# A hybrid decoder layer in one kernel: the order of a chunk's products, value tiles in halves of channels, transposes in eights, and one shifted tile

## The chip, the cores and the metric

The kernel runs on one core of a Trainium2 chip. Its time is device microseconds from launch to end; a lower time is better. The core has TensorE (PE, with the weight loads PEld beside it), VectorE (DVE), ScalarE (ACT), GpSimd (POOL), and SyncE (SP), which issues most of the DMAs. Each engine works its own instructions through in order and waits at semaphores for the others.

## The reference

One layer of a decoder trunk is computed for 2048 prompt tokens and for 8 separate sample tokens, all in float32. The normalised and modulated input `hn` goes through one input product whose columns are split into an LRU group (a convolution over 4 tokens, gates, a linear recurrence) and a group of gated linear attention (GLA) with 4 heads. Both are concatenated and go through one output product:

```python
hn = _rmsnorm(x, g_norm) * (1.0 + scale[:, None]) + shift[:, None]
z = hn @ w_in
xa, za, q, k, v, glr, zg = jnp.split(z, SPLITS, axis=-1)
...
def step(S, xs):
    qn, kn, vn, dl = xs
    o = jnp.einsum('bhck,bhkv->bhcv', qn, S)
    S = jnp.exp(dl[:, :, 0, :])[..., None] * S + jnp.einsum('bhck,bhcv->bhkv', kn, vn)
    return S, o
...
o = (o_intra + o_inter)...
mix = jnp.concatenate([y_lru, y_gla], axis=-1) @ w_out
x = x + gate[:, None] * mix
```

The model width is 1024, a head has 128 key and 256 value channels. The state `S` of a head (128 x 256) is carried from chunk to chunk: a chunk's output is the product inside the chunk (`o_intra`, masked attention times values) plus the query times the state (`o_inter`).

## The kernel before

**Numbers and products.** A float32 product is made of three products of rounded parts: high times high, high times low, low times high. So `project` (L661 to L663: projections with 128 weight columns at a time) and `value_mm` (L346 to L348: values, tokens on the partitions) issue three matmuls for each of the 8 channel tiles. The parts of `hn` are `hh` and `hl`. The weights come by SP in tiles `w`, three buffers in rotation (L293 issues such a load, split beforehand into parts); a load into a buffer waits on SP for the last instruction that read the buffer, and all later DMAs of SP wait behind it.

**Halves.** The 2048 tokens go in two halves of 1024. Half 0 runs to about 600 us, half 1 to about 1100 us, and the output product follows. In a half, each head (order 3, 0, 1, 2) has its key, value and query projections, and then segments of chunks of 128 tokens; between them run the LRU tiles. Between the halves `hn` of the second half must be put into `hh` and `hl`.

**Who sets the order.** A scheduler puts the instructions of each engine in order from the program's order and its own estimates. The program paces the GLA chunks by units of work (`tick`, `after`) and mixes small work into the projections: `drips` is a list of small steps, and `drip` takes one after every second channel tile of a projection.

**Accumulators.** PSUM gives `acc` four buffers (projections, values), `tp` two (transposes), and one bank each to `pkv` and `po`, the two results of a GLA chunk.

**The places of the change.**
- `gla_chunk` (L1059 on) is called 64 times, and 60 times with a carried state. It issues three products into `pkv` (keys times values: L1068 to L1070), three into `po` (masked attention `amh`, `aml` times values: L1072 to L1074) and the product of the query with the state, in float32, two passes (L1076). Then DVE adds `pkv` to the state (L1077), scales it (L1078) and copies `po` out (L1081). Before the first chunk of a segment, DVE makes the rests of the keys and of the attention, `kTl` (L1052) and `aml` (L1049), and scales the state (L1056).
- `values` (L933 on) multiplies 8 token tiles by a head's value weights, which lie in two `w` tiles, one for the channel tiles 0 to 3 and one for 4 to 7. In half 1 the last two token tiles are interleaved: both take the first half of the channels, then both the second. ACT (L957) and DVE (L958) take each result out. The next weights that SP loads are the query's.
- `next_hn` (L1428) calls `modulate`, which transposes two token tiles of the normalised second tokens for pairs of channel tiles (four transposes L197 for a pair), lets ACT (L199, L201) or DVE (L203) modulate, POOL round (L204, `hh`) and DVE subtract (L205, `hl`). `lru_last_a` puts these calls, one for each pair of channel tiles and each of four groups `g` of 256 tokens, into `drips`, so that they run inside the projections of the last LRU tile of half 0. Behind them come the sums of `hn` parts (L1491, L1495, L1500) for a Strassen product (L1559, about 600 to 620 us).
- `wq` (L471) holds the first query weights, a tile of the start.

Of the kernel before, what the change touches and what calls it, by code (L numbers as in the profile page):

```python
# [8 lines left out]
F32 = mybir.dt.float32  # L9
F32R = mybir.dt.float32r  # L10
# [4 lines left out]
P = 128  # L15
D = 1024
KT = D // P
# [4 lines left out]
DK = 128  # L22
DV = 256
# [3 lines left out]
XA, ZA, Q0, K0, V0, GLR, ZG = 0, 1024, 2048, 2560, 3072, 4096, 4112  # L27
# [11 lines left out]
HEADS = (3, 0, 1, 2)  # L39
# [15 lines left out]
def hybrid_kernel(ctx, tc, i, o):  # L55
# [7 lines left out]
    def acc():  # L63
        return psum.tile([P, 512], F32, tag="acc", name="acc", bufs=4)
# [41 lines left out]
    amh = cp.tile([P, 4, P], F32R, name="amh")  # L106
# [80 lines left out]
    def modulate(xt, g, kts):  # L187

        c = slice(g * 256, (g + 1) * 256)
        for k2 in range(kts[0], kts[1], 2):  # L190
            pt = tps().rearrange("p (k t) -> p k t", k=2)
            cg = slice(g % 2 * 256, g % 2 * 256 + 256)
            f = (fs4[(1, 2, 0)[k2 // 4 if g < 2 else 2]][:, k2 % 4:k2 % 4 + 2, cg] if g < 2 or k2 >= 4
                 else ra[k2 // 2][:, :, cg])
            for kt in range(2):
                for j in range(2):
                    PE.transpose(pt[:, kt, j * P:(j + 1) * P],  # L197
                                 xt[j][:, (k2 + kt) * P:(k2 + kt + 1) * P], ident)
            S.activation(f[:, 0], pt[:, 0], AF.Identity, scale=Gm[:, k2, 8:9], bias=Sh[:, k2, 8:9])  # L199
            if g < 3:  # L200
                S.activation(f[:, 1], pt[:, 1], AF.Identity, scale=Gm[:, k2 + 1, 8:9], bias=Sh[:, k2 + 1, 8:9])  # L201
            else:
                V.tensor_scalar(f[:, 1], pt[:, 1], Gm[:, k2 + 1, 8:9], Sh[:, k2 + 1, 8:9], op0=OP.mult, op1=OP.add)  # L203
            G.tensor_scalar(hh[:, k2:k2 + 2, c], f, 1.0, 0.0, op0=OP.mult, op1=OP.add)  # L204
            V.tensor_tensor(hl[:, k2:k2 + 2, c], f, hh[:, k2:k2 + 2, c].bitcast(F32), op=OP.subtract)  # L205
# [76 lines left out]
    def weights(col, n, k0=0, nk=KT, both=None, later=False, pieces=1):  # L282


        q = 48 if n == DV else 0
        c = slice(q, q + nk * n)
        if both is None:
            both = wp.tile([P, 2, 1088], F32R, tag="w", name="w", bufs=3)
        hi, lo = [both[:, j, c].rearrange("p (k n) -> p k n", n=n) for j in range(2)]
        known = (col, k0) in parts  # L290
        raw = None
        if known:
            SP.dma_start(both[:, :, c].bitcast(F32), parts[col, k0])  # L293
        else:
            raw = wp.tile([P, 1088], F32, tag="wr", name="wr")[:, :nk * n].rearrange("p (k n) -> p k n", n=n)
            for k in range(0, nk, nk // pieces):
                r = slice(k, k + nk // pieces)
                load = lambda r=r: SP.dma_start(raw[:, r], i["w_in"][
                    0, (k0 + r.start) * P:(k0 + r.stop) * P, col:col + n].rearrange("(k p) n -> p k n", p=P))
                loads.append(load) if k else load()  # L300
        split = []
        for k in range(0, nk, nk // pieces):
            r = slice(k, k + nk // pieces)
            split += [lambda r=r: S.copy(hi[:, r], raw[:, r]),
                      lambda r=r: V.tensor_tensor(lo[:, r], raw[:, r], hi[:, r].bitcast(F32), op=OP.subtract)]
        if not known:
            splits.extend(split)
            if not later:
                split_parts()
            parts[col, k0] = dpool.tile([P, 2, nk * n], F32, tag=f"w{col}_{k0}", name="parts")  # L310
            stores.append((parts[col, k0], both[:, :, c].bitcast(F32)))
            if not later:
                store_parts()
        return hi, lo, raw
# [28 lines left out]
    def value_mm(ps, c, w, n, kts):  # L343
        for kt in range(*kts):
            hi, lo, _ = w[kt // 4]
            PE.matmul(ps, hh[:, kt, c], hi[:, kt % 4], start=kt == 0, stop=False)  # L346
            PE.matmul(ps, hh[:, kt, c], lo[:, kt % 4], start=False, stop=False)  # L347
            PE.matmul(ps, hl[:, kt, c], hi[:, kt % 4], start=False, stop=kt == KT - 1)  # L348
            if kt % 2:
                drip()  # L350
# [86 lines left out]
    with tc.tile_pool(name="ada", bufs=1, side="right") as ap:  # L437
# [30 lines left out]
        xt45 = [xp.tile([P, TH + NS], F32, tag="xt", name="xt")[:, :D] for t in range(2)]  # L468
        for t in range(2):
            SP.dma_start(xt45[t], i["x_prompt"][0, (4 + t) * P:(5 + t) * P])  # L470
        wkq0.append(weights(Q0 + HEADS[0] * DK, DK, both=st.tile([P, 2, D], F32R, name="wq"), later=True))  # L471
        x67 = x_pair(2)
        for t in range(2):
            SP.dma_start(x67[t], i["x_prompt"][0, (6 + t) * P:(7 + t) * P])
# [458 lines left out]
    def values(half, h, w):  # L933
        first = h == HEADS[0]
        n = DV + (RANK if first else 0)
        vh, vl = new_values()
        turns = []
        for tt in range(8):
            if half == 1 and tt == first:
                with held(V) if first else ExitStack():  # L940
                    raw = raw_values(h, n)
            if tt == 4:
                while drips:
                    drip()
            if half == 0 or tt < 6:
                ps = acc()
                value_mm(ps[:, :n], slice(tt * P, (tt + 1) * P), w, n, (0, KT))
            elif tt == 6:
                both = [acc(), acc()]
                for k in (0, 4):  # L950
                    for m in range(2):
                        value_mm(both[m][:, :n], slice((6 + m) * P, (7 + m) * P), w, n, (k, k + 4))
                ps = both[0]
            else:
                ps = both[1]
            hi, lo = vh[tt // 4][:, tt % 4], vl[tt // 4][:, tt % 4]
            S.copy(hi, ps[:, :DV])  # L957
            V.tensor_tensor(lo, ps[:, :DV], hi.bitcast(F32), op=OP.subtract)  # L958
            if len(turns) == 3 or tt == 7 and turns:
                turns.pop(0)()  # L960
            if first:
                turns.append(low_rank(ps[:, DV:n], slice(0, P), tt * P))
            tick(0.5)
        if half == 1:
            turns.append(sample_values(h, raw, n))
        for f in turns:
            after(1, f, True)
        return vh, vl
# [90 lines left out]
    def gla_chunk(half, h, s, c, prep, run, v):  # L1059

        qi, _, f, _ = prep
        kT, on, ss = run
        first = half == 0 and s == 0 and c == 0
        t = slice(c * P, (c + 1) * P)
        pkv = psum.tile([P, 512], F32, tag="kv", name="pkv", bufs=1)[:, :DV]
        tt = SEGS[half][s][0] // P + c
        vh, vl = [x[tt // 4][:, tt % 4] for x in v]
        PE.matmul(pkv, kT[0][:, t], vh, start=True, stop=False)  # L1068
        PE.matmul(pkv, kT[0][:, t], vl, start=False, stop=False)
        PE.matmul(pkv, kT[1][:, t], vh, start=False, stop=True)  # L1070
        po = psum.tile([P, 512], F32, tag="o", name="po", bufs=1)[:, :DV]
        PE.matmul(po, amh[:, c], vh, start=True, stop=False)  # L1072
        PE.matmul(po, amh[:, c], vl, start=False, stop=False)
        PE.matmul(po, aml[:, c], vh, start=False, stop=first)  # L1074
        if not first:
            PE.matmul(po, qi[:, t], St[h], start=False, stop=True)  # L1076
            V.tensor_tensor(St[h], St[h], pkv, op=OP.add)  # L1077
            V.tensor_scalar(St[h], St[h], f[:, c + 1:c + 2], None, op0=OP.mult)  # L1078
        else:
            V.tensor_scalar(St[h], pkv, f[:, c + 1:c + 2], None, op0=OP.mult)  # L1080
        V.tensor_copy(on[:, c], po)  # L1081
        square_sum(xp, ss[:, c:c + 1], on[:, c], P, DV)
# [344 lines left out]

    def next_hn(xt, g, k):  # L1428

        modulate(xt[g], g, (k, k + 2))  # L1430
        if (g, k) == (1, 0):
            normalize(xp, xt[3])

    def lru_last_a(js):

        xa_load, xa_unit, za_load, za_unit = lru_units(0)
        xt = [hn_load(0)]
        lru(0, js[:-2])
        outw["stop"] = True
        lru(0, js[-2:-1])  # L1440
        t = xa_load(js[-1])
        za_load(t)
        flush_gla()
        while outw["busy"]:
            heapq.heappop(pend)[2]()
        open_sp()
        xt += [hn_load(1), hn_load(2), hn_load(3, False)]
        for s in range(2):
            xa_unit(t, s)
            za_unit(t, s)  # L1450
            for g in range(2 * s, 2 * s + 2):
                for k in range(0, KT, 2):
                    drips.append(lambda g=g, k=k: next_hn(xt, g, k))

    spx = ExitStack()
    sp_ = None
# [802 lines left out]
```

## Time and profile before

| | |
|---|---|
| time, median of 3 runs | 1449.03 us (1447.66 to 1450.63) |
| the profiled execution | 1449.01 us, of which the span 1447.2 us |
| PE busy | 1420.5 us, 98% |
| DVE busy | 1049.8 us, 73% |
| ACT busy | 690.2 us, 48% |
| POOL busy | 219.4 us, 15% |
| granted TensorE clock, mean | 0.997 |

The span is the time between the first and the last instruction. PE's matmuls overlap in the records: where a row has a duration of 0.28 us and the next starts 0.12 us later, 0.12 is what the matmul costs. I call the distance from one start to the next the step. A row of the timeline ends with the idle time before it and what ended that. A row of the waits names who waited, at which line, for whom.

### The profile page before, as it was taken

To read this page: it belongs to the slowest core of one execution; us is meant where nothing else is said; L and a number is where in the kernel's file an instruction comes from. 1 tells how busy PE (TensorE), PEld (TensorE's weight loads), DVE (VectorE), ACT (ScalarE), POOL (GpSimd) and SP (SyncE) were. 2 spreads that over 40 slices of the span, in tenths; PEclk is the share of its full clock that TensorE was granted. 3 is DMA by queue.
4 is the path that set the end of the run, shared out by engine and by line. 5 is a ranking of instruction groups with operands and counts; after the bars stand their busy time and mean duration, and the time that the engine had idled before them with its cause. 6 is when DMAs were issued, how large, how long until landed. Compare 5 with 4: busy or idle time off the path is not lost. (4 is left out here: it accounts for less than half of the span.)

```text
span 1447.2 us, 23571 instructions
## 1 busy us (share of the span) xinstructions
PE 1420.5 (98%) x8741; PEld 1248.7 (86%) x8741; DVE 1049.8 (73%) x2473; ACT 690.2 (48%) x1251; POOL 219.4 (15%) x364
## 2 busy tenths in 40 slices
PE   7999999999999999999999999999999999999998
PEld 6888989899898988878899999999998887778886
DVE  5757658776676688955458688596888986688886
ACT  4644544663445358624353454635567622144342
POOL 0200212122122013100111422333210000000000
PEclk9999999999999999999999999999999999999999
DMA  9755785874565546577844675655671767694453
GB/s 331 267 186 175 258 266 190 258 244 153 192 220 190 171 173 216 186 241 236 287 148 145 205 238 172 229 196 181 237 253 68 288 226 272 228 355 138 137 168 117
DMA packets 161753, 305.33 MB, mean 211 GB/s; under 512 B 12963, under 2 KB 91459, under 8 KB 159198
## 3 DMA queue, kind: packets, MB, share of 16 engines
q1 hardware_dynamic: 106837, 217.39, 44.1%
q0 software_dynamic: 22752, 70.44, 14.1%
q10 hardware_dynamic: 32048, 16.00, 3.7%
q8 instruction: 69, 1.13, 0.3%
q14 instruction: 47, 0.38, 0.1%
HBM read 188.51 MB, written 115.33 MB: 210 GB/s over the span
## 5 line engine op out<-in xcount | busy, mean ns | idle before, releaser
L661 PE MATMUL acc<-hh,w 128*128 128x512 f32 (+3 forms) x1112 | 385.7, 347 | 3.0 <-DMA w<-parts 1.8
L663 PE MATMUL acc<-hh,w 128*128 128x512 f32 (+3 forms) x1112 | 375.8, 338 | 0.0
L662 PE MATMUL acc<-hl,w 128*128 128x512 f32 (+3 forms) x1112 | 375.1, 337 | 0.2 <-DVE hl L205 0.2
L661 PEld LDWEIGHTS acc<-hh,w 128*128 128x128 f32 x1112 | 209.2, 188 | 21.7 <-DVE f L1005 1.6
L662 PEld LDWEIGHTS acc<-hl,w 128*128 128x128 f32 x1112 | 209.3, 188 | 16.7 <-DVE hl L205 0.5
L663 PEld LDWEIGHTS acc<-hh,w 128*128 128x128 f32 x1112 | 209.1, 188 | 16.5
L1845 PE MATMUL acc<-w,a 128*128 128x512 f32 (+1 forms) x792 | 184.8, 386 | 0.0
L1845 PEld LDWEIGHTS acc<-w,a 128*128 128x128 f32 x792 | 146.8, 188 | 33.2 <-issue 3.4
L346 PE MATMUL acc<-w,hh 128*128 128x256 f32 (+1 forms) x508 | 143.8, 283 | 0.1
L348 PE MATMUL acc<-w,hl 128*128 128x256 f32 (+1 forms) x508 | 142.8, 281 | 0.2 <-DVE hl L228 0.2
L347 PE MATMUL acc<-w,hh 128*128 128x256 f32 (+1 forms) x508 | 142.7, 281 | 0.0
L1845 PE MATMUL tp<-w,a 128*128 128x512 f32 x564 | 136.3, 391 | 0.0
L1845 PEld LDWEIGHTS tp<-w,a 128*128 128x128 f32 x564 | 105.2, 188 | 27.2 <-issue 5.1
L346 PEld LDWEIGHTS acc<-w,hh 128*128 128x128 f32 x508 | 95.6, 188 | 1.3 <-ACT zs L1129 0.4
L348 PEld LDWEIGHTS acc<-w,hl 128*128 128x128 f32 x508 | 96.0, 189 | 0.4 <-DVE hl L228 0.4
L347 PEld LDWEIGHTS acc<-w,hh 128*128 128x128 f32 x508 | 95.5, 188 | 0.2
L1129 ACT ACTIVATE zs<-acc 128x512 f32<-128x512 f32 (+3 forms) x70 | 34.4, 491 | 110.1 <-PE acc L663 105.0
L1695 ACT CAST a<-s 128x512 fp32r<-128x512 f32 x61 | 36.5, 620 | 95.1 <-issue 34.5
L1278 DVE SCALAR_TENSOR_TENSOR cv<-xa,vecT,cv 128x512 f32<-128x512 f32 (+2 forms) x120 | 76.6, 641 | 5.5 <-ACT cv L1276 5.1
L1130 DVE SCALAR_TENSOR_TENSOR zs<-zs,acc 128x512 f32<-128x512 f32 (+3 forms) x70 | 38.5, 550 | 45.7 <-ACT zs L1129 45.7
L957 ACT CAST vh<-acc 128x256 fp32r<-128x256 f32 x56 | 20.5, 370 | 85.9 <-PE acc L348 68.0
L958 DVE TENSOR_TENSOR vl<-acc,vh 128x256 fp32r<-128x256 f32 x56 | 23.4, 420 | 47.1 <-ACT vh L957 46.9
(409 smaller groups left out, 2745.2 us busy)
## 6 DMA issues: line engine op xcount, KB each, us to landing
parts<-w SPq DMA_DIRECT2D x37, 1024.0 KB
w<-parts SPq DMA_DIRECT2D x28, 1024.0 KB
wr<-in_w_in_dram SPq DMA_DIRECT2D x38, 512.0 KB
a<-mixd SPq DMA_DIRECT2D x63, 256.0 KB
w<-wd SPq DMA_DIRECT2D x12, 1024.0 KB
w<-twd SPq DMA_DIRECT2D x20, 512.0 KB
mixd<-zs ACTq DMA_DIRECT2D x34, 256.0 KB
wada<-in_w_ada_dram SPq DMA_DIRECT2D x16, 512.0 KB
```

What stands on the lines that cost most here:

```text
L346: PE.matmul(ps, hh[:, kt, c], hi[:, kt % 4], start=kt == 0, stop=False)
L347: PE.matmul(ps, hh[:, kt, c], lo[:, kt % 4], start=False, stop=False)
L348: PE.matmul(ps, hl[:, kt, c], hi[:, kt % 4], start=False, stop=kt == KT - 1)
L661: PE.matmul(ps[:, :n], hi[:, kt], a, start=kt == 0, stop=False)
L662: PE.matmul(ps[:, :n], hi[:, kt], b, start=False, stop=False)
L663: PE.matmul(ps[:, :n], lo[:, kt], a, start=False, stop=kt == KT - 1)
L958: V.tensor_tensor(lo, ps[:, :DV], hi.bitcast(F32), op=OP.subtract)
L1129: S.activation(z, ps, AF.Tanh, scale=0.5)
L1130: V.scalar_tensor_tensor(z, z, 1.0, ps, op0=OP.add, op1=OP.mult)
L1278: V.scalar_tensor_tensor(cv[:, cq], xa[:, cq.start + k:cq.stop + k], cw[k], cv[:, cq], op0=OP.mult, op1=OP.add)
L1695: S.copy(t[:, 0, k], (low(t) if src is None else src)[:, k])
L1845: PE.matmul(ps, t[:, u, k], w[:, v, k, c], start=(q < 3 or ps is own) and (k, u, v) == (0, 0, 0), stop=(k, u) == (3, 1), skip_group_check= ...
```

## The change

Four edits, independent of each other.

1. In `gla_chunk` the state's product opens the accumulation in `po` and stands before the products of `pkv`; the attention's products close it.
2. In `values` of half 1 the last three token tiles instead of the last two are interleaved by halves of the channels.
3. `next_hn` handles four channel tiles in a call (eight transposes) instead of two, and an empty step follows each in `drips`, so that as many steps stand in the list as before.
4. The tile of the first query weights is 56 floats longer, and the weights begin behind these 56 floats (224 bytes), which shifts them and the tiles allocated after them in the start's pool.

```diff
-        wkq0.append(weights(Q0 + HEADS[0] * DK, DK, both=st.tile([P, 2, D], F32R, name="wq"), later=True))
+        wkq0.append(weights(Q0 + HEADS[0] * DK, DK, both=st.tile([P, 2 * D + 56], F32R, name="wq")[:, 56:].rearrange("p (j n) -> p j n", j=2), later=True))
...
-            if half == 0 or tt < 6:
+            if half == 0 or tt < 5:
                 ps = acc()
                 value_mm(ps[:, :n], slice(tt * P, (tt + 1) * P), w, n, (0, KT))
-            elif tt == 6:
-                both = [acc(), acc()]
-                for k in (0, 4):
-                    for m in range(2):
-                        value_mm(both[m][:, :n], slice((6 + m) * P, (7 + m) * P), w, n, (k, k + 4))
-                ps = both[0]
             else:
-                ps = both[1]
+                if tt == 5:
+                    three = [acc() for _ in range(3)]
+                    for k in (0, 4):
+                        for m in range(3):
+                            value_mm(three[m][:, :n], slice((5 + m) * P, (6 + m) * P), w, n, (k, k + 4))
+                ps = three[tt - 5]
...
+        po = psum.tile([P, 512], F32, tag="o", name="po", bufs=1)[:, :DV]
+        if not first:
+            PE.matmul(po, qi[:, t], St[h], start=True, stop=False)
         PE.matmul(pkv, kT[0][:, t], vh, start=True, stop=False)
         PE.matmul(pkv, kT[0][:, t], vl, start=False, stop=False)
         PE.matmul(pkv, kT[1][:, t], vh, start=False, stop=True)
-        po = psum.tile([P, 512], F32, tag="o", name="po", bufs=1)[:, :DV]
-        PE.matmul(po, amh[:, c], vh, start=True, stop=False)
+        PE.matmul(po, amh[:, c], vh, start=first, stop=False)
         PE.matmul(po, amh[:, c], vl, start=False, stop=False)
-        PE.matmul(po, aml[:, c], vh, start=False, stop=first)
+        PE.matmul(po, aml[:, c], vh, start=False, stop=True)
         if not first:
-            PE.matmul(po, qi[:, t], St[h], start=False, stop=True)
             V.tensor_tensor(St[h], St[h], pkv, op=OP.add)
...
-        modulate(xt[g], g, (k, k + 2))
+        modulate(xt[g], g, (k, k + 4))
...
-                for k in range(0, KT, 2):
-                    drips.append(lambda g=g, k=k: next_hn(xt, g, k))
+                for k in range(0, KT, 4):
+                    drips.extend([lambda g=g, k=k: next_hn(xt, g, k), lambda: None])
```

PE, one chunk of half 0. Before (`S_117` is the state, `xb` the query, L1042 the next transposes of the attention):

```order
L1068 MATMUL pkv<-vh,kTh 128x256
L1069 MATMUL pkv<-vl,kTh 128x256
L1070 MATMUL pkv<-vh,kTl 128x256
L1072 MATMUL po<-vh,amh 128x256
L1073 MATMUL po<-vl,amh 128x256
L1074 MATMUL po<-vh,aml 128x256
L1076 MATMUL po<-S_117,xb 128x256
```

After, with the line numbers of the changed kernel (L1069 there is the state's product):

```order
L1069 MATMUL po<-S_117,xb 128x256
L1070 MATMUL pkv<-vh,kTh 128x256
L1071 MATMUL pkv<-vl,kTh 128x256
L1072 MATMUL pkv<-vh,kTl 128x256
L1073 MATMUL po<-vh,amh 128x256
L1074 MATMUL po<-vl,amh 128x256
L1075 MATMUL po<-vh,aml 128x256
```

The state's product moved from the end of the chunk's seven to its head, and with it the first use of `po`.

DVE, during the last LRU tile of half 0, up to the sum L1130 that frees an accumulator near 577 us (L1278 is the convolution, L147 to L153 a reciprocal root in short steps). Before; ahead of these rows stand an L1278 and an L205:

```order
L1278 SCALAR_TENSOR_TENSOR cv<-xa,vecT,cv 128x512
L147 TENSOR_SCALAR rs_x<-ss 128x2
L1278 SCALAR_TENSOR_TENSOR cv<-xa,vecT,cv 128x512
L148 TENSOR_SCALAR rs_t<-rs_x 128x2
L1385 COPY xa<-xac 128x3
L149 TENSOR_SCALAR rs_y<-rs_t 128x2
L151 TENSOR_TENSOR rs_t<-rs_y 128x2
L205 TENSOR_TENSOR hl<-fs_5824,hh 128x2x256
L152 SCALAR_TENSOR_TENSOR rs_t<-rs_t,rs_x 128x2
L153 SCALAR_TENSOR_TENSOR rs_y<-rs_t,rs_y 128x2
L1130 SCALAR_TENSOR_TENSOR zs<-zs,acc 128x512
```

After; ahead of these rows stand an L1278, an L205, an L1278 and another L205:

```order
L1278 SCALAR_TENSOR_TENSOR cv<-xa,vecT,cv 128x512
L147 TENSOR_SCALAR rs_x<-ss 128x2
L1385 COPY xa<-xac 128x3
L148 TENSOR_SCALAR rs_t<-rs_x 128x2
L149 TENSOR_SCALAR rs_y<-rs_t 128x2
L151 TENSOR_TENSOR rs_t<-rs_y 128x2
L152 SCALAR_TENSOR_TENSOR rs_t<-rs_t,rs_x 128x2
L153 SCALAR_TENSOR_TENSOR rs_y<-rs_t,rs_y 128x2
L205 TENSOR_TENSOR hl<-fs_5828,hh 128x2x256
L151 TENSOR_TENSOR rs_t<-rs_y 128x2
L152 SCALAR_TENSOR_TENSOR rs_t<-rs_t,rs_x 128x2
L1130 SCALAR_TENSOR_TENSOR zs<-zs,acc 128x512
```

Between the first of the three L1278 and L1130 now stand three L205 instead of two, and more of the short steps.

DVE, the end of the same turns, about 586 to 596 us. Before:

```order
L203 TENSOR_SCALAR ra<-tp,Gm,Sh 128x256
L205 TENSOR_TENSOR hl<-ra,hh 128x2x256
L1130 SCALAR_TENSOR_TENSOR zs<-zs,acc 128x256
L203 TENSOR_SCALAR ra<-tp,Gm,Sh 128x256
L205 TENSOR_TENSOR hl<-ra,hh 128x2x256
L203 TENSOR_SCALAR fs_5823<-tp,Gm,Sh 128x256
L205 TENSOR_TENSOR hl<-fs_5823,hh 128x2x256
L1130 SCALAR_TENSOR_TENSOR zs<-zs,acc 128x256
L203 TENSOR_SCALAR fs_5823<-tp,Gm,Sh 128x256
L1500 TENSOR_TENSOR fs_5823<-fs_5823,ra 128x1024
L205 TENSOR_TENSOR hl<-fs_5823,hh 128x2x256
L1330 SCALAR_TENSOR_TENSOR tx<-tx,cv 128x1024
```

After:

```order
L203 TENSOR_SCALAR ra<-tp,Gm,Sh 128x256 x2
L205 TENSOR_TENSOR hl<-ra,hh 128x2x256 x2
L1130 SCALAR_TENSOR_TENSOR zs<-zs,acc 128x256
L203 TENSOR_SCALAR fs_5823<-tp,Gm,Sh 128x256 x2
L205 TENSOR_TENSOR hl<-fs_5823,hh 128x2x256 x2
L1130 SCALAR_TENSOR_TENSOR zs<-zs,acc 128x256
L1330 SCALAR_TENSOR_TENSOR tx<-tx,cv 128x1024
L1500 TENSOR_TENSOR fs_5823<-fs_5823,ra 128x1024 x2
```

Pairs of L203 and L205 that alternated now stand two by two, and both L1500 stand together behind L1330.

## The prediction

> **What bounds the kernel now.** I read the page first, then the waits of PE, then the timelines of the places that the change touches. The page, with PE's share, its slices and its granted clock:
>
> ```profile
> span 1447.2 us, 23571 instructions
> PE 1420.5 (98%) x8741; PEld 1248.7 (86%) x8741; DVE 1049.8 (73%) x2473; ACT 690.2 (48%) x1251; POOL 219.4 (15%) x364
> PE   7999999999999999999999999999999999999998
> PEclk9999999999999999999999999999999999999999
> ```
>
> PE is the bound from end to end. The change leaves PE's instructions as many and as large as they were, so it can move the time in two ways only: what PE waits for, and how fast a matmul runs. The profiled execution took 1449.01 us (span 1447.2), 0.02 from the median of the runs, 1449.03; my sum is made against 1449.0 and needs no correction. A difference under 0.2% (2.9 us) can hardly be told from none.
>
> These rows of PE's waits (us in total, times, longest) are those that the change can reach; the last is that of PE's weight loads:
>
> ```profile
> PE acc L661 <- DMA w<-parts: 1.8, 2, 1.3
> PE acc L1559 <- DVE so L1495: 1.4, 2, 1.2
> PE po L1072 <- DVE on L1081: 0.9, 2, 0.7
> PE acc L661 <- DVE zs L1130: 0.9, 1, 0.9
> PE acc L1559 <- DVE ra L1495: 0.8, 1, 0.8
> PE pkv L1070 <- DVE kTl L1052: 0.8, 3, 0.3
> PE acc L662 <- DVE hl L205: 0.2, 1, 0.2
> PEld po L1072 <- DVE on L1081: 3.3, 10, 1.0
> ```
>
> They are small: 6.8 us of idle without the last row. No outcome of tens of microseconds is in sight unless the change makes a wait that isn't there.
>
> **The value tiles (values, half 1).** The queue SP loads the next query weights (L293) into a buffer of `w` that the first half of the channels of the value weights still holds; it waits for the last matmul that reads it. Two of these loads, and what PE does when it reaches them:
>
> ```profile
> 818.06 0.52 SPq L293 DMA_DIRECT2D w<-parts  x1
> 825.80 0.33 PE L662 MATMUL acc<-hl,w 128*128 128x384 f32 x1
> 825.97 0.34 PE L663 MATMUL acc<-hh,w 128*128 128x384 f32 x1
> 827.60 0.41 PE L661 MATMUL acc<-hh,w 128*128 128x384 f32 x1 [1.29 <-DMA w<-parts]
> ...
> 907.99 0.52 SPq L293 DMA_DIRECT2D w<-parts  x1
> 915.90 0.34 PE L663 MATMUL acc<-hh,w 128*128 128x384 f32 x1
> 916.77 0.41 PE L661 MATMUL acc<-hh,w 128*128 128x384 f32 x1 [0.53 <-DMA w<-parts]
> ```
>
> PE's step there is 0.17 (825.80 to 825.97), so the stalls cost 827.60 - 825.97 - 0.17 = 1.46 and 916.77 - 915.90 - 0.17 = 0.70. With two tiles in halves, the first half of the channels is read for the last time 24 matmuls (4 channel tiles x 3 x 2 tiles) before the end of the values; with three tiles, 36. The load may go out 12 matmuls earlier. A matmul of 128x256 steps 0.12 (753.53 to 753.65 in the fence below; 264 wide there), so 1.4 us. The landing lies 9.5 and 8.8 us behind the issue; if it moves with the issue, the first stall shrinks to about 0.1 and the second is gone: **-2.1**. The other two heads show no such wait and gain nothing. The bounds: 0, if the transfer meets others and lands no earlier, and -2.2. The three evictions that now come close together (L957, L958) feed chunks that begin much later, and four accumulators are enough for three open ones, so they cost nothing; if they were late, the next projection would wait for an accumulator, at most the 0.4 us of one L958.
>
> **The state's product first (gla_chunk).** Sixty chunks issue it, in two passes. A chunk without waits, then the second chunk of a segment, then the first chunk of the next segment:
>
> ```profile
> 752.97 0.59 PE L1076 MATMUL po<-S,xb 128*128 128x256 f32 x2
> 753.53 0.29 PE L662 MATMUL acc<-hl,w 128*128 128x264 f32 x1
> 753.65 0.28 PE L663 MATMUL acc<-hh,w 128*128 128x264 f32 x1
> ...
> 756.54 0.28 PE L1070 MATMUL pkv<-vh,kTl 128*128 128x256 f32 x1
> 756.95 0.38 PE L1072 MATMUL po<-vh,amh 128*128 128x256 f32 x1
> ...
> 852.61 0.28 PE L1069 MATMUL pkv<-vl,kTh 128*128 128x256 f32 x1
> 853.15 0.38 PE L1070 MATMUL pkv<-vh,kTl 128*128 128x256 f32 x1 [0.27 <-DVE kTl L1052]
> ```
> ```profile
> 756.48 0.42 DVE L1081 COPY on<-po 128x256 f32<-128x256 f32 x1
> 851.64 0.34 DVE L1056 TENSOR_SCALAR S<-S,f 128x256 f32<-128x256 f32 x1
> 852.55 0.55 DVE L1052 TENSOR_TENSOR kTl<-tp,kTh 128x384 fp32r<-128x384 f32 x1
> ```
>
> The product costs 753.53 - 752.97 - 0.12 = 0.44 us wherever it stands. What moves is when PE asks for its inputs. The bank `po` is single: it is free when the copy L1081 of the chunk before has ended. Now three products of `pkv` (3 x 0.12 = 0.36 us) run ahead of that demand; afterwards none. At 756.54 PE waits until the copy's end (756.48 + 0.42 = 756.90): step 0.41, so 0.29 lost. It will wait 0.36 longer. That place occurs once in each of four heads (756, 847, 936, 1025 us): **+1.4**. Against it, at the first chunk of a second segment (852, 941, 1031 us) PE waits for kTl: 853.15 - 852.61 - 0.12 = 0.42, with further steps of about 0.4 for kTh and aml; there S is ready (851.64 + 0.34 = 851.98, while pkv begins at 852.38), so 0.44 us of product come ahead and fill those gaps, and the amh group no longer has to wait: net -0.46 a head, **-1.4**. Of the other chunks the waits above name few: 2 matmuls and 10 weight loads in 64 chunks waited for L1081. In half 0 the timelines show S and the copy ready at least 0.3 us before `pkv` begins, so these cost nothing but about 0.2 at 506 us, where DVE's order changes; a handful of chunks in half 1 that already stand late gain 0.1 to 0.2 each in the same way as at 852, by my estimate -0.8. Together 1.4 - 1.4 + 0.2 - 0.8 = **-0.6**, between -2.0 (the gaps filled, no new wait) and +1.8 (no gap filled, four longer waits).
>
> **The turns of next_hn in eights.** As many transposes in fewer, larger groups. The stall at 577 us, and the four waits of DVE for POOL's cast near the end of these turns:
>
> ```profile
> 576.85 0.60 PE L197 MATMUL tp<-ident,xst 128*128 128x128 f32 x4
> 578.37 0.39 PE L661 MATMUL acc<-hh,w 128*128 128x256 f32 x1 [0.92 <-DVE zs L1130]
> ...
> 576.76 0.68 DVE L205 TENSOR_TENSOR hl<-fs,hh 128x512 fp32r<-128x512 f32 x1
> 577.36 0.15 DVE L152 SCALAR_TENSOR_TENSOR rs_t<-rs_t,rs_x 128x2 f32<-128x2 f32 x1
> 577.63 0.69 DVE L1130 SCALAR_TENSOR_TENSOR zs<-zs,acc 128x512 f32<-128x512 f32 x1
> ...
> 587.78 0.69 DVE L205 TENSOR_TENSOR hl<-ra,hh 128x512 fp32r<-128x512 f32 x1 [0.81 <-POOL hh L204]
> 590.07 0.69 DVE L205 TENSOR_TENSOR hl<-ra,hh 128x512 fp32r<-128x512 f32 x1 [0.81 <-POOL hh L204]
> 592.03 0.69 DVE L205 TENSOR_TENSOR hl<-fs,hh 128x512 fp32r<-128x512 f32 x1 [0.81 <-POOL hh L204]
> 595.15 0.69 DVE L205 TENSOR_TENSOR hl<-fs,hh 128x512 fp32r<-128x512 f32 x1 [0.51 <-POOL hh L204]
> ```
>
> First the loss. PE at 577 waits for an accumulator that L1130 frees. In the new order one more L205 (0.68) and two or three short steps of the reciprocal root (0.15 each, with the gaps between them 0.2) stand ahead of that L1130 on DVE: it ends about 1.1 us later, and the stall grows by that. Then the gain. DVE's four waits are 0.81 x 3 + 0.51 = 2.94 us. Afterwards two L203 stand together, then two L205: the second L203 and POOL's second cast run inside the first wait, which halves the waits (-1.5), and the last group of transposes leaves one interleaving turn (about 1.9 us) earlier. So DVE's chain into the Strassen sums (L1500, L1491, L1495), for which PE waits from 612 to 620, comes about 2.2 us earlier. PE's idle for so, ra and hl is 1.4 + 0.8 + 0.2 = 2.4, and each of the four restarts adds about 0.17 (1.46 against the 1.29 above): 3.0, all shorter than 2.2 each. I take 2.8 of it: 1.1 - 2.8 = **-1.7**. Bounds: +1.1 (nothing regained) and -3.0 (all regained, the first stall unchanged).
>
> [...] Here PEclk reads 9 in every slice, stalls included. [...]
>
> **The first query weights.** Forty-eight matmuls read them, and run slightly longer than their like:
>
> ```profile
> L661 PE MATMUL acc<-hh,wq 128*128 128x512 f32 x16 | 6.5, 405 | 0.0
> L661 PE MATMUL acc<-hh,w 128*128 128x512 f32 x408 | 163.0, 400 | 0.0
> ```
>
> If the shift of 56 floats ends that, 48 x 5 ns = 0.24: **-0.3** (between 0 and -0.4).
>
> **The sum.** -2.1 - 0.6 - 1.7 - 0.3 = -4.7; 1449.0 - 4.7 = 1444.3, and I say 1444.5.
>
> **The rivals.**
> 1. *The loads land no earlier.* The 2.1 stays. For it: DMA is busy at this time, and the landing takes 9 us for 0.5 MB. Against: the issue waits for PE and for nothing else. Result 1449.0 - 2.6 = 1446.4, within 0.2%. Chance 0.10.
> 2. *The turns in eights lose.* The stall at 577 grows, and the late waits stay because DVE's later sums, not the turns, set them: +1.1 in place of -1.7. For it: the loss stands on DVE's order, while the gain passes through some 20 DVE steps. Result 1449.0 - 2.1 - 0.6 + 1.1 - 0.3 = 1447.1, within 0.2%. Chance 0.14.
> 3. *State first waits in the ordinary chunk: slower.* The three `pkv` products cover 0.36 us of the copy L1081 and of S; if DVE comes just in time in half 1, all 32 chunks there lose that cover: 32 x 0.36 = 11.5, and 1449.0 - 4.1 + 11.5 = 1456. From 20 chunks on (20 x 0.36 - 4.1 = 3.1) the kernel is slower by over 0.2%. For it: ten weight loads wait for L1081 already. Against: that is 10 of 64. Chance 0.10.
> 4. [...] Chance 0.03. [...]
>
> **How the numbers follow.** The forecast has 0.63. A slow mishap (3) has 0.10, the three that stay near 1447 have 0.27. From below, every bound at its best gives 1449.0 - 2.2 - 2.0 - 3.0 - 0.4 = 1441.4; it is unlikely that all meet, so the range begins at 1441.8. Above it takes in rivals 1, 2 and 4 and a first part of 3, to 1449.0. The likeliest case alone lies between 1442 and 1446. Faster by over 0.2% (below 1446.1): 0.63 and a little of rival 1, so 0.64; within: 0.25; slower: 0.11.
>
> **What will show it.** The row of PE's waits for w<-parts falls from 1.8 to below 0.4, and SP issues its loads 1.4 us earlier against the end of the values. PE's wait for L1130 near 577 grows to about 2; those for so, ra and hl fall below 0.6 together. The wait of po for L1081 now stands at the state's product, four times near 0.65; that for kTl is gone. L661 with wq reads 400. I am wrong if the state's product shows waits in many more chunks, or if the late sums still hold PE from 612 to 620 us.

## The result and the profile after

The changed kernel takes 1446.3 us (median of 22 runs, 1444.65 to 1449.62) against 1448.38 us of the kernel before in runs beside it (22 runs, 1446.3 to 1450.63): a ratio of 0.9986, 95% interval 0.9979 to 0.9992. That is 2.0 us (1.2 to 3.0) faster, in the direction of the forecast and less than half its size. The forecast of 1444.5 was made against 1449.0, the median of three early runs; against the 22 it would read 1443.9.

The page of the changed kernel, the same rows as before. The profiled execution took 1447.76 us, 1.5 above the median: it is one of the slower ones.

```profile
span 1445.9 us, 23584 instructions
PE 1419.8 (98%) x8741; PEld 1249.8 (86%) x8741; DVE 1050.5 (73%) x2473; ACT 690.0 (48%) x1251; POOL 219.0 (15%) x364
PEclk9999999999999999999999999999999999999999
```

PE's waits in it (us in total, times, longest):

```profile
PE po L1069 <- DVE on L1081: 3.4, 6, 1.0
...
PE acc L1559 <- ACT acc L1573: 1.8, 1, 1.8
...
PE acc L1559 <- DVE ra L1495: 1.0, 1, 1.0
...
PE acc L661 <- DMA w<-parts: 0.8, 2, 0.4
...
PE tp L197 <- DVE xst L181: 0.6, 2, 0.4
...
PE tp L197 <- ACT fs L201: 0.3, 1, 0.3
PE tp L197 <- ACT ra L201: 0.3, 1, 0.3
```

The waits for so, hl, kTl and the one at 577 us are gone. In their places stand a wait of `po` for the copy L1081, 3.4 us where it was 0.9; a wait of 1.8 for a copy of ACT, L1573, that no row of before had; and waits of the transposes themselves.

Two profiles of one kernel differ, so I read them by stages. PE runs 8741 matmuls in each; I compare the start of the n-th matmul with the start of the n-th in the profile of before, and a stage's figure is how much that difference changes from the stage's begin to its end. "Half 0" is from 288 to 540 us (16 chunks, no other edit of the change falls there), "turns" from 540 to 628 us, with the lag that PE has gathered since 540 at 612 us, "half 1" from 721 to 1072 us. Parts: w the shifted first query weights, c the state's product first, v the value tiles, t the turns in eights. Microseconds, below zero earlier:

| kernel (parts) | ratio of the times (95%) | half 0 | turns | lag at 612 | half 1 | idle of PE for w<-parts in half 1 |
|---|---|---|---|---|---|---|
| before | 1 | 0 | 0 | 0 | 0 | 1.8 |
| changed (w c v t) | 0.9986 (0.9979, 0.9992) | -0.60 | +0.31 | +2.24 | -0.09 | 0.8 |
| e1_chunk (c) | 1.0006 (0.9997, 1.0015) | -0.60 | +0.40 | +0.37 | +3.47 | 2.9 |
| e2_values (v) | 0.9998 (0.9989, 1.0007) | +0.03 | +0.01 | -0.01 | -2.06 | 0 |
| e3_turns (t) | 1.0001 (0.9992, 1.001) | +0.04 | +0.15 | +3.32 | +0.41 | 1.7 |
| e4_wq (w) | 1.0002 (0.9994, 1.0011) | 0.00 | -0.23 | -0.27 | -0.26 | 1.7 |
| e5_no_turns (w c v) | 0.9993 (0.9985, 1.0002) | -0.57 | +0.38 | +0.33 | -1.60 | 0 |
| f1_no_values (w c t) | 1.0001 (0.9991, 1.001) | -0.60 | +0.51 | +3.66 | -1.24 | 0 |
| f2_no_chunk (w v t) | 0.9987 (0.9978, 0.9996) | 0.00 | +0.04 | +3.23 | -0.71 | 0.3 |
| f4_chunk_values (c v) | 0.9993 (0.9984, 1.0002) | -0.60 | +0.22 | +0.19 | -1.11 | 0 |
| e6_turns_queue | 0.9986 (0.9977, 0.9994) | -0.57 | +0.81 | -0.45 | -0.86 | 0 |
| e7_chunk_part | 0.9986 (0.9977, 0.9995) | -0.57 | -0.05 | +1.87 | -1.63 | 0 |
| e8_all | 0.9987 (0.9979, 0.9996) | -0.57 | +0.20 | +0.36 | -1.91 | 0 |
| f3_four | 1.0004 (0.9995, 1.0013) | -0.58 | +0.02 | +1.96 | +1.41 | 0 |

One of the eleven runs of f3 took 2350.4 us at a mean granted clock of 0.556, and its ratio leaves that run out.

No single run's interval settles a part. Put together, the nine kernels that hold some of the four parts as they are (changed, e1 to e5, f1, f2, f4) give, in a fit in which the parts add, w -0.2 (plus or minus 0.9), c +0.3 (0.8), v -1.3 (0.8), t -0.4 (0.8) us.

That the parts add is an assumption: the four sum to -1.6, where -2.0 was measured. The five kernels with the value tiles and the turns (changed, f2, e6, e7, e8) stand at 0.9986 to 0.9987, the three with the value tiles and without the turns (e2, e5, f4) at 0.9993 to 0.9998; the means are 1.2 us apart, plus or minus about 0.9. The two with the turns and without the value tiles (e3, f1) stand at 1.0001. So the times leave room for a gain of the turns beside the value tiles. The stages show none, and no run here settles it.

### The profile page after: what moved, and what is told of

It is laid out like the page before. It is cut to its first block, busy times and chain, and to the rows that moved or that the text cites. A ratio compares the mean times of both kernels' runs of the same rounds, so it can differ in the third digit from the quotient of the medians.

```text
span 1445.9 us, 23584 instructions
## 1 busy us (share of the span) xinstructions
PE 1419.8 (98%) x8741; PEld 1249.8 (86%) x8741; DVE 1050.5 (73%) x2473; ACT 690.0 (48%) x1251; POOL 219.0 (15%) x364
## 4 chain that ended last, share of the span: by engine, by line
PE 78%; DVE 9%; issue 4%; DMA 4%; ACT 3%; POOL 1%; SPq 0%; DVEq 0%; POOLq 0%; ACTq 0%
PE acc L1845 12%; PE acc L661 10%; PE acc L663 10%; PE acc L662 10%; PE tp L1845 9%; PE acc L1559 6%; PE acc L346 3%; PE acc L347 3%; PE acc L348 3%; PE po L1069 2%; DMA w<-parts 1%; PE acc L1315 1%; PE tp L1163 1%; PE acc L1317 1%; PE acc L1316 1%
## 5 line engine op out<-in xcount | busy, mean ns | idle before, releaser
L661 PE MATMUL acc<-hh,w 128*128 128x512 f32 (+3 forms) x1112 | 377.4, 339 | 1.0 <-DMA w<-parts 0.8
L663 PE MATMUL acc<-hh,w 128*128 128x512 f32 (+3 forms) x1112 | 374.7, 337 | 0.0
L663 PEld LDWEIGHTS acc<-hh,w 128*128 128x128 f32 x1112 | 209.1, 188 | 15.9
L1278 DVE SCALAR_TENSOR_TENSOR cv<-xa,vecT,cv 128x512 f32<-128x512 f32 (+2 forms) x120 | 76.6, 641 | 3.5 <-ACT cv L1276 2.9
L1130 DVE SCALAR_TENSOR_TENSOR zs<-zs,acc 128x512 f32<-128x512 f32 (+3 forms) x70 | 38.4, 549 | 48.1 <-ACT zs L1129 48.1
## 6 DMA issues: line engine op xcount, KB each, us to landing
parts<-w SPq DMA_DIRECT2D x37, 1024.0 KB
w<-parts SPq DMA_DIRECT2D x28, 1024.0 KB
w<-wd SPq DMA_DIRECT2D x12, 1024.0 KB
```

The source lines that it names most:

```text
L661: PE.matmul(ps[:, :n], hi[:, kt], a, start=kt == 0, stop=False)
L663: PE.matmul(ps[:, :n], lo[:, kt], a, start=False, stop=kt == KT - 1)
L1130: V.scalar_tensor_tensor(z, z, 1.0, ps, op0=OP.add, op1=OP.mult)
L1278: V.scalar_tensor_tensor(cv[:, cq], xa[:, cq.start + k:cq.stop + k], cw[k], cv[:, cq], op0=OP.mult, op1=OP.add)
```

## The experiments

**Each part alone.** Of the diff, e1 holds the hunk of `gla_chunk`, e2 that of `values`, e3 those of `next_hn` and `lru_last_a`, e4 that of `wq`.

> The state's product first alone. Theory from the two traces: an ordinary chunk of half 0 gets cheaper by some 24 ns (1614 to 1590, 1502 to 1478 from the last matmul before it to the second behind it), the wait for the copy L1081 at the second chunk of each head's first segment grows from about 0.3 to about 0.65-0.7 (four heads, +1.5), the waits for kTl (3 x 0.43) go, and two or three new waits for L1081 of 0.3 appear: in all between -0.8 and +0.3 us against before, half 0 gaining 0.5 to 1.0 and half 1 losing as much. The prediction's own figure: -0.6, all from half 1, half 0 unchanged.

Measured: 1449.35 us, 1.0006 (0.9997 to 1.0015). The stages bear the theory out on half 0, which the prediction had at nothing: every kernel with the state first is 0.57 to 0.60 us earlier over the 16 chunks, every one without it 0.04 off at most. That is 0.036 us a chunk, or 1.0 us if all 28 chunks with a carried state in half 0 gain as much. How it comes, in a chunk of before and the same chunk of the changed kernel:

```profile
333.79 0.40 PE L663 MATMUL acc<-hh,w 128*128 128x512 f32 x1
334.02 0.28 PE L1068 MATMUL pkv<-vh,kTh 128*128 128x256 f32 x1
...
334.74 0.60 PE L1076 MATMUL po<-S,xb 128*128 128x256 f32 x2
334.99 0.58 PE L661 MATMUL acc<-hh,w 128*128 128x512 f32 x1
335.40 0.40 PE L662 MATMUL acc<-hl,w 128*128 128x512 f32 x1
335.64 0.40 PE L663 MATMUL acc<-hh,w 128*128 128x512 f32 x1
335.87 0.40 PE L661 MATMUL acc<-hh,w 128*128 128x512 f32 x1
```
```profile
333.20 0.39 PE L663 MATMUL acc<-hh,w 128*128 128x512 f32 x1
333.43 0.59 PE L1069 MATMUL po<-S,xb 128*128 128x256 f32 x2
333.67 0.47 PE L1070 MATMUL pkv<-vh,kTh 128*128 128x256 f32 x1
333.98 0.28 PE L1071 MATMUL pkv<-vl,kTh 128*128 128x256 f32 x1
...
334.56 0.39 PE L661 MATMUL acc<-hh,w 128*128 128x512 f32 x1
334.79 0.40 PE L662 MATMUL acc<-hl,w 128*128 128x512 f32 x1
335.02 0.39 PE L663 MATMUL acc<-hh,w 128*128 128x512 f32 x1
```

From the last L663 ahead to the second matmul behind it took 335.40 - 333.79 = 1.61 before and 334.79 - 333.20 = 1.59 now, and the next matmuls behind the chunk, which step 0.23 to 0.24 before, step 0.23 now. It is a change of step, not of a wait, and no row of waits has it.

Half 1 of e1 is 3.5 us later, mostly for a wait that this part doesn't touch: the query weights came late (2.46 us of wait), and a fall of the granted clock to 0.51 followed (the section on the hardware below).

> Three value tiles in halves alone. Prediction: the waits for w<-parts fall from 1.46 and 0.70 to 0.1 and 0, -2.1 us. Theory from the two traces: the loads go out 1.4 us earlier but land up to 0.5-1.5 us later after their issue, so that one or two waits of 0.4 to 0.6 remain, also in a head that had none: -1.1 us.

Measured: 1448.08 us, 0.9998 (0.9989 to 1.0007). In its profile no wait for w<-parts is left and half 1 is 2.06 us earlier, what the prediction had said. The times of this run do not bear it out: -0.3 us, with -1.6 at the end of the interval.

> The turns in eights alone. Prediction: -1.7 us. Theory from the two traces: the waits for so, hl and zs (about 3.2 with restarts) go, but ACT issues the DMA of L675 ahead of the copy L1573, waits there for DVE's L1352 and holds PE 1.9 us at about 607; PE further waits about 0.4 four times for the transposes' buffers and for xst; net +0.3 us (between -0.3 and +0.9), no gain.

Measured: 1448.37 us, 1.0001 (0.9992 to 1.001); the turns end 0.15 us later. The theory fits, and the order of work that it names is there. On ACT before, and in the changed kernel:

```profile
606.57 0.58 ACT L1573 COPY acc<-acc 128x512 f32<-128x512 f32 x1
609.00 1.09 ACTq L675 DMA_DIRECT2D mixd<-zs  x2
```
```profile
603.81 1.04 ACT L1494 CAST hh<-ra 128x1024 fp32r<-128x1024 f32 x1
607.22 1.10 ACTq L675 DMA_DIRECT2D mixd<-zs  x2
608.36 0.57 ACT L1573 COPY acc<-acc 128x512 f32<-128x512 f32 x1 [3.51 <-DVE zs L1352]
```

The copy and the two DMA issues have changed places. The DMAs wait for DVE's L1352, and the copy that PE waits for now stands behind them in ACT's queue: ACT is idle ahead of it for 3.51 us, and PE waits 1.8. All kernels with the turns have this wait, except e6 and e8, which change the queue.

> The shifted first query weights alone. Both theories: the 48 matmuls that read wq fall from 395-405 to 390-400 ns, -0.24 us, below what the times can tell; the rest of the trace is as before, so this run also shows how far two profiles of the same order differ. Rival: the shift changes nothing in these matmuls, 0.0.

Measured: 1448.63 us, 1.0002 (0.9994 to 1.0011). The shift does what it was to do, and as little as that; in the changed kernel:

```profile
L661 PE MATMUL acc<-hh,wq 128*128 128x512 f32 x16 | 6.4, 401 | 0.0
L663 PE MATMUL acc<-hh,wq 128*128 128x512 f32 x16 | 6.3, 392 | 0.0
L662 PE MATMUL acc<-hl,wq 128*128 128x512 f32 x16 | 6.2, 390 | 0.0
```

This run, with before's order on every engine, also shows how far two profiles differ by themselves: up to 0.3 us in a stage of the table, 0.7 in the first 63 us and 0.9 from there to 288 us.

**The queue of ACT and the place of DVE.** If the wait for L1573 is the price of the turns, it can be taken away: e5 is the changed kernel without the hunks of the turns, e6 the changed kernel with the two DMAs issued by POOL:

```diff
-        (G if half == 1 and ct in LRU_TILES[3][1:] else S).dma_start(
+        (G if ct in LRU_TILES[3][1:] and (half == 1 or ct == LRU_TILES[3][-1]) else S).dma_start(
```

> The change without the turns in eights. If the turns lose (theory: ACT issues L675 before the copy L1573, a stall of 1.8 us of idle on PE, after which the granted clock fell to 0.64 for 4.5 us in the run of the turns alone, though not in the profile of the changed kernel), this kernel is 0.3 to 1.5 us faster than the changed kernel, 2.3 to 3.5 below before. The prediction (the turns gain 1.7) has it 1.7 us slower than the changed kernel, about level with before. In the trace L1573 stands ahead of L675 and PE's wait for it is gone; the waits for so and hl are back (2.1 us).

> The changed kernel, but the two output DMAs of the last LRU tile of half 0 are issued by POOL instead of ACT, so that no copy of ACT stands behind them. Theory: PE's wait for ACT's L1573 (1.9 us) is gone, the gain of the turns appears as predicted (so and hl waits gone, only ra left), 1.9 to 3 us faster than the changed kernel, 4 to 5 below before. Rival: the stall has another cause, for instance DVE's chain, and PE waits as long at the next step; then level with the changed kernel, 2 below before.

Measured: e5 1447.34 us, 0.9993 (0.9985 to 1.0002); e6 1446.43 us, 0.9986 (0.9977 to 0.9994). By the times e5 is neither faster than the changed kernel, as the theory had it, nor level with before: it lies between, within the error of both. e6 is level with the changed kernel, as its rival has it. In the profile of e6 the wait for L1573 is gone and PE reaches 612 us 0.45 ahead instead of 2.24 behind; by 628 us it is 0.81 behind. Its waits:

```profile
PE acc L1559 <- DVE hl L1495: 1.2, 1, 1.2
...
PE acc L1559 <- DVE ra L1495: 0.4, 1, 0.4
PE acc L1559 <- DVE so L1495: 0.4, 1, 0.4
```

And the stretch from 600 to 622 us (length, then busy time of PE, PEld, DVE, ACT, POOL, with instructions; the granted clock is the third number from the end), of before, of the changed kernel and of e6, and for e6 the part behind its last wait:

```profile
600.00:622.00 22.00, 19.74 (x85) 15.27 (x84) 22.00 (x23) 10.74 (x14) 0.60 (x1) 1.00 0.79 263
```
```profile
600.00:622.00 22.00, 19.28 (x84) 15.24 (x83) 20.85 (x22) 10.05 (x13) 0.60 (x1) 1.00 0.78 262
```
```profile
600.00:622.00 22.00, 19.99 (x79) 15.36 (x78) 19.03 (x21) 8.49 (x12) 2.13 (x3) 0.92 0.72 251
...
618.10:621.51 3.41, 3.41 (x9) 2.63 (x8) 0.89 (x1) 0.00 (x0) 0.00 (x0) 0.50 0.61 216
```

Before, DVE works through all 22.00 us of it, and after, until PE has caught up at 620. In e6 a part of the waits of PE came back at the sums (2.0 us of idle, where the changed kernel has 1.8 + 1.0), but the 0.81 is not their work alone: behind the last wait the granted clock was 0.50 for 3.41 us, eight steps of 0.43 in place of 0.23, which cost 1.6 us. So e6 doesn't show by itself that a lead gains nothing. The kernels without a slow stretch there tell more. From 600 to 628 us the changed kernel, e7 and f3, which have the wait of 1.8, fall back 0.15 us; e8 below, which has not, gains 0.16; e6 with 1.6 for the slow clock taken off gains 0.34. So in that stretch the wait of 1.8 us is worth 0.3 to 0.5, not the 1.9 to 3 that the theory of e6 had: most of it comes back at the sums, which wait for DVE. The other side shows the same: e3, f1 and f2 come to 612 us 3.2 to 3.7 us late (the wait for L1573, and then a slow clock: 0.64 in e3, 0.62 in f1 and f2), and at 628 us they are 0.04 to 0.5 late.

**The second chunks.** In the changed kernel PE waits for the copy L1081 with the state's product, as foretold:

```profile
755.28 0.28 PE L663 MATMUL acc<-hh,w 128*128 128x264 f32 x1
756.05 0.70 PE L1069 MATMUL po<-S,xb 128*128 128x256 f32 x2 [0.49 <-DVE on L1081]
```

The step is 0.77, so 0.65 lost, where 0.29 was lost before. This is the second chunk of the first segment (c = 1). In the other three heads the wait stands at the third chunk (c = 2), though the prediction and the expectations speak of the second in all four. e7 puts the product back to the end in the chunks with c = 1 of half 1, so it reaches one of the four long waits, and those at the second chunks of the second segments; e8 joins that to e6.

```diff
+        ahead = not first and not (half == 1 and c == 1)
+        if ahead:
+            po = psum.tile([P, 512], F32, tag="o", name="po", bufs=1)[:, :DV]
+            PE.matmul(po, qi[:, t], St[h], start=True, stop=False)
         PE.matmul(pkv, kT[0][:, t], vh, start=True, stop=False)
...
+        if not first and not ahead:
+            PE.matmul(po, qi[:, t], St[h], start=False, stop=True)
```

> The changed kernel, but the state's product is kept last in the second chunk of each segment of half 1, where PE waits for the copy L1081. Theory: the four waits of 0.65 to 0.84 fall to about 0.3 to 0.4, those of about 0.3 and 1.19 at the second chunks of the second segments fall by 0.3 each, the waits for kTl stay away: 2.0 to 2.5 us faster than the changed kernel. Rival: what PE gains there it loses at the next wait for DVE, less than 0.7 us faster.

> Both edits together: the two output DMAs on POOL and the state's product last in the second chunks of half 1. If both theories hold, their gains add: 4 to 5 us faster than the changed kernel, 6 to 7 below before, about 1442. If only the queue counts: 1.9 to 3 below the changed kernel; if neither, level with it.

Measured: e7 1446.62 us, 0.9986 (0.9977 to 0.9995); e8 1447.19 us, 0.9987 (0.9979 to 0.9996). Neither gains the 2.0 to 2.5 that was expected, but they do not decide between theory and rival, for the edit leaves three of the four long waits where they were. The waits of e7, then the first of these three in the changed kernel and in e7:

```profile
PE po L1076 <- DVE on L1086: 1.9, 3, 1.2
...
PE po L1070 <- DVE on L1086: 1.5, 3, 0.5
```
```profile
846.58 0.70 PE L1069 MATMUL po<-S,xb 128*128 128x256 f32 x2 [0.52 <-DVE on L1081]
```
```profile
845.08 0.70 PE L1070 MATMUL po<-S,xb 128*128 128x256 f32 x2 [0.51 <-DVE on L1086]
```

L1086 is the copy, L1076 there the attention's product and L1070 the state's product in the kernel's own numbers. The 1.5 of L1070 are the three waits that the edit does not reach. The 1.9 of L1076 stand where it does, at the second chunks of the second segments; there the waits did not fall but are 0.35, 1.24 and 0.31, where the changed kernel has 0.17, 1.03 and none listed. In the first head, the one place of the four that the edit reaches, 0.29 is lost as before the change, and a wait of 0.35 for the state S appears at the next chunk. Half 1, without what the query weights account for, is 0.5 and 0.2 us later than before in e7 and e8, and 0.5 to 1.3, 0.9 in the mean, in the kernels with the state first in every chunk: a gain of about 0.5, no larger than the spread.

**The parts taken out.** f1 is the changed kernel without the hunk of `values`, f2 without that of `gla_chunk`; f4 is the kernel before with those two hunks.

> The change without the value tiles: shifted weights, state first, turns in eights. If the value tiles bring the gain (in the profiles without them PE's waits for w<-parts come to 1.9 to 3.2 us, once with a fall of the clock behind; with them to 0 to 1.1), this kernel is 1.5 to 3 us slower than the changed kernel, level with before within 0.8. If the gain comes from the sum of small things (half 0's chunks), it is 1 to 1.5 us below before.

> The change without the state's product first. By the traces state first gains 0.75 us in half 0 (24 to 30 ns in each of 28 chunks) and loses 0.5 to 1.0 in half 1: this kernel is level with the changed kernel within 0.7. By the prediction it is 0.6 slower than it; if the longer waits for the copy L1081 counted in full (four of 0.65 to 0.84 and a third of 0.3 twice), it would be 1 us faster.

> State first and value tiles together, without the shift and the turns. If the turns and the shift are worth nothing, this is level with the changed kernel, 1.5 to 2.5 below before. If the two parts only add as they measured alone (+0.9 and -0.3), it is 0.6 above before.

Measured: f1 1448.05 us, 1.0001 (0.9991 to 1.001); f2 1446.69 us, 0.9987 (0.9978 to 0.9996); f4 1447.26 us, 0.9993 (0.9984 to 1.0002). Without the value tiles the gain is gone; without the state first it is all there. State first and value tiles together lie between the two answers foretold for f4. The profile of f1 complicates the picture: it has no wait for w<-parts at all. Without the value tiles that idle came to 1.8, 2.9, 1.7, 1.7 and 0 us in five profiles, with them (three tiles, four in f3) to 0.8, 0, 0, 0, 0, 0, 0.3, 0 and 0 in nine. With two tiles the wait at the second of the two places was 0.53 us in before, 1.69 in e3 and 2.46 in e1: it moves from run to run by more than the stall of 0.70 there, and with the edit a stall is rare; its mean worth by the profiles is about 1.6 - 0.1 = 1.5 us plus the restarts, by the times 1.3 (plus or minus 0.8).

**More of the same.** f3 interleaves four value tiles:

```diff
-            if half == 0 or tt < 5:
+            if half == 0 or tt < 4:
...
-                    three = [acc() for _ in range(3)]
+                    four = [acc() for _ in range(4)]
```

> The changed kernel with the last four value tiles in halves of channels. The load of the query weights goes out another 1.4 us earlier (48 matmuls before the end of the values instead of 36). If PE's rest wait for w<-parts (0 to 1.1 us, different from run to run) still costs, 0 to 1 us faster than the changed kernel and no wait for w<-parts in the profile; rival: the four accumulators are all taken, the next projection waits for their evictions (L957, L958) for 0.4 to 1 us in four heads, 1 to 3 us slower than the changed kernel.

Measured: 1449.11 us, 1.0004 (0.9995 to 1.0013). The rival holds, with one difference of place: not the next projection waits, but the four tiles themselves, for the eviction of tiles before them:

```profile
PE acc L346 <- DVE vl L957: 2.5, 3, 1.2
```

Three tiles leave one of the four accumulators for what is being taken out; four leave none. No version here is faster than the changed kernel beyond the error.

## Why the prediction was right, and where it was not

- **Value tiles, -2.1.** Right in its mechanism, and the part without which the gain is gone (f1). Without the turns it gives -0.3 to -1.0 by the times (e2, e5, f4). The loads go out 1.4 us earlier, the stalls of 1.46 and 0.70 shrink (by the steps, the changed kernel's profile has 0.49 at the first, none at the second, and 0.61 in a head that had none). The size in the mean is nearer 1.5, for the prediction took one profile's landings, 9.5 and 8.8 us, as fixed. Rival 1 (the loads land no earlier) has fallen; its 0.5 MB should read 1 MB, as the page lists these loads (1024.0 KB).
- **State first, -0.6.** The sum was about right by the stages, by luck, for both halves of it were wrong. Half 0 was costed at nothing but a loss of 0.2 and gives about 1.0, by a shorter step behind the float32 product. In half 1 the four waits grew as foretold (0.65 to 0.83 for 0.29 to 0.41; one at the second chunk of its segment, three at the third), the waits for kTl went as foretold, but two waits of 0.3 for L1081 came up at the second chunks of second segments, and the 0.86 at 949 us became 1.19; the -0.8 that I estimated for "a handful of chunks" did not come. Half 1 loses some 0.5 us net: with what the idle for the query weights differs put back (and the slow clock of e1), the stage is 0.9 us later in the six kernels with the state first in all chunks (0.5 to 1.3) and 0.4 in the four without it, e2, e3, e4 and f2 (-0.2 to 1.0). By the times the part is worth +0.3, plus or minus 0.8, so the sign of the whole isn't settled. Rival 3 (waits in the ordinary chunk) has fallen: 6 waits, not 20.
- **Turns in eights, -1.7.** This is the step that failed: "DVE's chain into the Strassen sums ... comes about 2.2 us earlier", and "I take 2.8 of it". The halved waits for POOL are there, as foretold: the two that are left are 0.36 each, where four were 2.94 in sum.

```profile
587.63 1.69 DVE L205 TENSOR_TENSOR hl<-ra,hh 128x512 fp32r<-128x512 f32 x2 [0.36 <-POOL hh L204]
...
590.92 1.69 DVE L205 TENSOR_TENSOR hl<-fs,hh 128x512 fp32r<-128x512 f32 x2 [0.36 <-POOL hh L204]
```

But the loss that the prediction booked on PE's account alone, L1130 near 578 us coming later, is DVE's too, and has to come off the gain of the same chain. It was sized at 1.1. L1130 starts at 578.64 for 577.63, and since the changed kernel had brought a lead of 1.2 along from 540 us, it comes 2.2 later in its stage. Of that DVE still has 1.1 at 583 us (L205 at 583.22 for 583.29). At the end of the chain the first L1495 that writes ra starts at 617.40 for 619.17, 1.8 earlier, of which again 1.2 was brought along: 0.6 is what the turns gave DVE, not 2.2 (0.4 to 1.2 in the eight profiles with the turns). The rest of the difference I can't place row by row. The stall at 577, on the other hand, did not grow but went: PE has waits of the transposes for their buffers and for L181 in its place (0.46, 0.42, 0.52 and 0.46 us by the steps, 1.9 in all for 1.0). And the new order put L675 ahead of L1573 on ACT, an exchange of which the prediction says nothing: it speaks of PE's and DVE's order there, not of ACT's. That exchange looked like the culprit and is a small part of it, 0.3 to 0.5 of its 1.8 us; the rest goes into the sums all the same. Net +0.1 by the stages (the mean of the stage is +0.25 in changed, e3, f1 and f2, and +0.13 in before, e1, e2, e4, e5 and f4), -0.4 plus or minus 0.8 by the times if the parts add, and about -1.2 beside the value tiles if they do not: that this part gains nothing is what the stages say, and it stays open. Rival 2 (the late waits stay because DVE's later sums set them, 1447.1) had the mechanism; it came to about nothing rather than +1.1.
- **First query weights, -0.3.** 4 ns on each of 48 matmuls, 0.2 us.
- **The sum.** By the stages and profiles -1.5 - 0.5 + 0.1 - 0.2 = -2.1, measured -2.0 (-3.0 to -1.2). That these agree to 0.1 is luck, for each term has an error of some tenths. Of the forecast's -4.7, the 1.7 of the turns and 0.6 of the value tiles were not there, by the same account. The direction held. So did the range, which was drawn to take in the rivals and says little for the sum; the case that came is the one within 0.2%, to which I gave 0.25.
- **Rival 4, the clock.** Its chance of 0.03 and its place in the range were my estimate: no run shows the granted clock falling at 577 us, and in the changed kernel's profile it is 1.00 from 577 to 582 us and from 600 to 622. What the runs showed in its place is a fall at the sums in e3 (0.64), f1 and f2 (0.62) and e6 (0.50), and one in half 1 of e1 (0.51), where 3.2 us of slow steps cost 1.6.

## What to carry to other kernels

Before a stall is booked as a gain, look at the engine that is waited for: where it is busy through the whole stretch (22.00 of 22 us here), its work is most of the bound, and removing a wait of 1.8 us gained 0.3 to 0.5. A loss of order on such an engine comes off its own later gain. When an edit reorders work, compare all queues for exchanges between a DMA issue that waits and a copy that somebody waits for. And a stall on a transfer has a spread (waits of 0.53, 1.69 and 2.46 us at one place here): an edit that sends it 1.4 us earlier is worth the mean over landings, for which one profile is a poor guide. Before an edit is made at "the second chunk", read in every head which chunk the wait stands at: here it was another one in three of four.

## What the hardware showed beside that

The granted clock fell behind waits of 2.46 us (e1), 1.8 us (e3), and 1.2 and 0.4 us together (e6). In e1 the wait was for the query weights. First PE's timeline, then the same place in the windows (length, busy times of the engines, and the granted clock as the third number from the end):

```profile
917.65 0.41 PE L661 MATMUL acc<-hh,w 128*128 128x384 f32 x1 [2.46 <-DMA w<-parts]
...
919.14 0.52 PE L662 MATMUL acc<-hl,w 128*128 128x384 f32 x1
919.46 0.52 PE L663 MATMUL acc<-hh,w 128*128 128x384 f32 x1
```
```profile
918.60:922.00 3.40, 3.40 (x12) 3.40 (x12) 0.67 (x2) 0.00 (x0) 3.17 (x6) 0.51 0.62 199
```

The step is 0.32 where it is 0.17 at full clock, for about 3.2 us from 918.8 on, more than a microsecond after PE had taken up work again. It cost 1.6 us (ten steps longer by 0.15, two by 0.05) on top of the 2.63 of the stall itself. In e3, behind the 1.8 us for L1573:

```profile
610.00:614.50 4.50, 4.50 (x13) 3.58 (x14) 4.50 (x5) 1.57 (x3) 0.00 (x0) 0.64 0.92 312
```

f1 and f2 show 0.62 in the same place; the changed kernel, e7 and f3 have the same stall of 1.8 us there and a clock of 1.00 behind it, and so has e3 behind its wait of 1.69 us for the query weights (1.00 from 918.60 to 922.00 us). In e6 no single wait was longer than 1.2 us. These are the 3.41 us ahead of its slow stretch, with waits of 1.2 and 0.4 in them; PE was busy for 1.78:

```profile
614.69:618.10 3.41, 1.78 (x7) 0.97 (x6) 3.41 (x5) 1.08 (x2) 0.13 (x1) 1.00 1.04 389
```

In the same length ahead of the fall PE was busy for 1.62 us in e3 (fall at 611.24) and 1.04 in e1 (at 918.69). So PE was idle for 1.63 us (e6, in two waits), 1.79 (e3) and 2.37 (e1) of the 3.41 us ahead of a fall, while the stall of 1.8 us in the changed kernel, e7 and f3 had no fall behind it. What decides it isn't shown here. In e1 the page of slices hides the fall, as does the mean clock of 0.998.
